# Moving each output store between the two weight loads of a later group in a batched matrix multiplication

**Chip, cores, metric.** One core of one Trainium2 chip. The metric is the device time of one execution in microseconds (us). The kernel before takes 518.66 us (median of six runs, 518.55 to 519.05).

## The reference

```python
x      = randn(8, 16, 256, 512)   # float32
weight = randn(8, 16, 512, 384)   # float32
return np.matmul(x, weight)       # 128 products of 256x512 by 512x384
```

## The kernel before

It works on 32 groups of four products. For each group SP issues two weight loads of 1.57 MB and one x load of 2.10 MB, four groups ahead, and one store of 1.57 MB. (PE also has "weight loads" of its own, called PE loads in the code below: they bring one operand from SBUF into PE.) ACT casts x to bf16, PE transposes it, DVE copies the transposed x out of PSUM and casts the weights, PE multiplies, ACT copies the result out of PSUM.

```python
def load(e, t, U, s):                          # group n
    for d in range(2):                         # two weight loads
        e.wait_ge(w_cast, ...)                 # the slot's weights of group n-2 are cast
        e.dma_start(w_sb[slot][:], ...).then_inc(w_in[slot], 16)
    e.wait_ge(x_cast, ...)                     # x of group n-2 is cast
    e.dma_start(x_sb[s % XS][:], ...).then_inc(x_in[s % XS], 16)

def store(e, t, U, s, pieces=1):
    e.wait_ge(o_copied, ...)                   # the output of group n is copied out
    e.dma_start(out=dram[:, rows], in_=out_sb[s % OS][:, rows]).then_inc(o_out[s % OS], 16)

def on_sync(e):
    for n in range(LAG): load(e, 0, NG, n)     # LAG = 4
    with e.Fori(0, rounds) as t:
        for s in range(U):
            load(e, t, U, LAG + s)             # w, w, x of group n+4
            store(e, t, U, s)                  # store of group n
    ...

def multiply(e, t, U, s):                      # PE, one group
    for q in range(T):                         # 16 transposes, each with its PE load
        e.wait_ge(x_cast, n * T + (q + 1))
        ...
    for q in range(T):                         # 128 multiplications: 32 columns of x,
        for rr in range(2):                    # loaded into PE, by 384 columns of
            for ko in range(KO):               # weights, each with a PE load of its own
                for i in range(G):
                    ins = e.matmul(po[...][mine, rr, :N], x_t[...], w_bf[...][:, ko, :], ...)
```

## Time and profile before

| | before |
|---|---|
| time | 518.66 us |
| span of the profiled execution | 517.2 us |
| busy share: DMA, DVE, PE, ACT | 99.3%, 64%, 59%, 46% |
| moved | 218.1 MB, 429 GB/s in the steady part |

The 16 DMA engines are busy nearly throughout, and no compute engine is. The lines of the profile stand in the prediction. "DMA share" in a row of windows is the mean busy share of the 16 engines, so a single engine working alone shows as 1/16, or 0.06.

### The profile page before, as it was taken

The numbers are of one execution on the slowest core, as the hardware profiler recorded it, in microseconds if no ns is written. First come the engines' busy times: TensorE is split into PE (matmuls) and PEld (weight loads), VectorE is DVE, ScalarE is ACT, GpSimd is POOL, SyncE is SP. The second block draws the span as 40 slices with busy tenths as digits, with TensorE's granted clock in tenths as the row PEclk, the third lists the DMA queues.
The fourth block names the chain that finished last, engine by engine and source line by source line (L and its number), as shares of the span: only waits on it lengthen the run. The fifth ranks groups of instructions, "written<-read, shape, count | busy, mean of one in ns | idle before, by whom it ended". The sixth has DMA issues, their size and how long they took to land.

```text
span 517.2 us, 11523 instructions
## 1 busy us (share of the span) xinstructions
PE 306.6 (59%) x4608; PEld 200.6 (39%) x4608; DVE 332.8 (64%) x384; ACT 236.7 (46%) x264; POOL 0.7 (0%) x6
## 2 busy tenths in 40 slices
PE   0478776556665457645577554776446765467752
PEld 0345444334443334433344332444324443244431
DVE  3698875667556676556675566855658656676550
ACT  0465564443644436435355354454444544544441
POOL 0000000000000000000000000000000000000000
PEclk9998877878777887878777778877788877778777
DMA  8999999999999999999999999999999999999996
GB/s 340 430 423 424 424 432 426 429 428 430 432 427 427 427 428 432 429 427 430 426 431 431 426 429 430 427 432 427 427 429 429 427 433 425 430 428 430 429 428 251
DMA packets 18869, 218.18 MB, mean 422 GB/s; under 512 B 2096, under 2 KB 2096, under 8 KB 2608
## 3 DMA queue, kind: packets, MB, share of 16 engines
q1 hardware_dynamic: 18864, 218.11, 99.3%
q8 instruction: 3, 0.05, 0.0%
q14 instruction: 2, 0.02, 0.0%
HBM read 167.77 MB, written 50.33 MB: 422 GB/s over the span
## 4 chain that ended last, share of the span: by engine, by line
DMA 81%; ACT 10%; PE 4%; issue 3%; ACTq 0%; SPq 0%
DMA x_sb<-in_x_dram 81%; ACT x_bf L132 9%; PE po L180 2%; PE pt L166 1%; ACTq L130 0%; ACT out_sb L194 0%; SPq L111 0%; SPq L103 0%; ACT L132 0%; ACTq L193 0%; SPq L282 0%; SPq L55 0%
## 5 line engine op out<-in xcount | busy, mean ns | idle before, releaser
L147 DVE CAST w_bf<-w_sb 64x1536 bf16<-64x1536 f32 x256 | 244.4, 955 | 47.2 <-DMA w_sb<-in_weight_dram 38.5
L166 PE MATMUL pt<-identity,x_bf 128*128 128x128 f32 x512 | 123.7, 425 | 199.3 <-ACT x_bf L132 199.1
L180 PE MATMUL po<-w_bf,x_t 128*32 128x384 bf16 x4096 | 185.1, 342 | 1.0 <-issue 1.0
L166 PEld LDWEIGHTS pt<-identity,x_bf 128*128 128x128 f32 x512 | 91.8, 216 | 232.1 <-issue 218.3
L194 ACT COPY out_sb<-po 128x768 f32<-128x768 f32 x128 | 102.2, 798 | 147.2 <-PE po L180 147.2
L153 DVE COPY x_t<-pt 128x1024 bf16<-128x1024 bf16 x128 | 88.4, 691 | 122.3 <-PE pt L166 121.8
L132 ACT CAST x_bf<-x_sb 128x1024 bf16<-128x1024 f32 x128 | 124.4, 1042 | 80.9 <-DMA x_sb<-in_x_dram 80.8
L180 PEld LDWEIGHTS po<-w_bf,x_t 128*32 128x32 bf16 x4096 | 108.8, 101 | 73.8 <-issue 14.2
L132 ACT ACT_TABLE_LOAD x8 | 10.3, 1283 | 42.9 <-DMA x_sb<-in_x_dram 42.9
masks.py:199 POOL TENSOR_SCALAR_AFFINE_SELECT identity<-identity 128x128 f32<-128x128 f32 x1 | 0.3, 292 | 0.2 <-POOL identity L200 0.2
L200 POOL MEMSET identity<- 128x128 f32 x1 | 0.2, 204 | 0.5 <-SPq L55 0.5
L271 POOL MEMSET const-bfloat16-1.0<- 128x1 bf16 x1 | 0.1, 101 | 0.0
L271 POOL MEMSET const-uint8-127<- 128x1 uint8 x1 | 0.1, 101 | 0.0
L271 POOL MEMSET const-float32-0.0<- 128x1 f32 x1 | 0.1, 98 | 0.2 <-issue 0.2
L271 POOL MEMSET const-float32-1.0<- 128x1 f32 x1 | 0.1, 98 | 0.0
## 6 DMA issues: line engine op xcount, KB each, us to landing
w_sb<-in_weight_dram SPq DMA_DIRECT2D x64, 1536.0 KB, 27.5
x_sb<-in_x_dram SPq DMA_DIRECT2D x32, 2048.0 KB, 27.5
out_dram<-out_sb SPq DMA_DIRECT2D x31, 1536.0 KB, 30.7
out_dram<-out_sb SPq DMA_DIRECT2D x4, 384.0 KB, 5.9
```

Source lines behind the costliest of these rows:

```text
L132: e.copy(out=x_bf[s % BS][:, rows], in_=x_sb[s % XS][:, rows].rearrange("p r (q s c) -> p r s q c", s=S, c=KO),).then_inc(x_cast, 1)
L147: e.tensor_copy(out=w_bf[(s * G + d * D + a) % WBS][h * HP : (h + 1) * HP], in_=w_sb[slot][a * HP : (a + 1) * HP, h * KO : (h + 1) * KO, : ...
L153: e.tensor_copy(out=x_t[s % TS][:, 2 * q : 2 * q + 2], in_=pt[(s * T + q) % PT][:].bitcast(bf16),).then_inc(t_copied, 1)
L166: ins = e.transpose(pt[(s * T + q) % PT][:, rr, h, :], words[:, 2 * q + rr, h :: KO // 2], identity[:],)
L180: ins = e.matmul(po[(s * T + q) % PO][mine, rr, :N], x_t[s % TS][:, 2 * q + rr, ko // 2, mine, ko % 2], w_bf[(s * G + i) % WBS][:, ko, :], ...
L194: e.copy(out=out_sb[s % OS][:, 2 * q : 2 * q + 2, :], in_=po[(s * T + q) % PO][:, :, :N],).then_inc(o_copied, 1)
L200: e.memset(identity[:], 0.0).then_inc(id_done, 1)
L271: nc = _bacc.Bacc("TRN2", target_bir_lowering=False, num_devices=1)
```

## The change

The intent: a store should stand in the queue with a weight load on either side, and no x load next to it. So the loader is split, and the store goes between the two weight loads of the group issued beside it. For the last groups the old order stays.

```diff
-    def load(e, t, U, s):
+    def load_w(e, t, U, s, d):        # one weight load
+    def load_x(e, t, U, s):           # the x load
 ...
-        rounds = (NG - LAG) // U
+        rounds = (NG - LAG) // U - 1
         with e.Fori(0, rounds) as t:
             for s in range(U):
-                load(e, t, U, LAG + s)
+                load_w(e, t, U, LAG + s, 0)
                 store(e, t, U, s)
+                load_w(e, t, U, LAG + s, 1)
+                load_x(e, t, U, LAG + s)
         for n in range(rounds * U, NG):
+            late = n + LAG >= NG - 1          # then the store comes after the loads, as before
 ...
```

More of the change, by code (lines that the diff above doesn't have):

```diff
@@ L94 @@
     BIAS = 8
-    def load(e, t, U, s):
+    def load_w(e, t, U, s, d):
         n = t * U + s
-        for d in range(G // D):
-            slot = (s * (G // D) + d) % WS
-            if not isinstance(n, int) or n >= 2:
-                e.wait_ge(w_cast, n * (G * S) + ((d + 1) * D * S - 2 * G * S))
-            e.dma_start(
-                w_sb[slot][:],
-                w_rows[bass.ds(n * (G * K) + d * (D * K), D * K)].rearrange(
-                    "(p k) n -> p k n", k=S * KO
-                ),
-            ).then_inc(w_in[slot], 16)
+        slot = (s * (G // D) + d) % WS
+        if not isinstance(n, int) or n >= 2:
+            e.wait_ge(w_cast, n * (G * S) + ((d + 1) * D * S - 2 * G * S))
+        e.dma_start(
+            w_sb[slot][:],
+            w_rows[bass.ds(n * (G * K) + d * (D * K), D * K)].rearrange(
+                "(p k) n -> p k n", k=S * KO
+            ),
+        ).then_inc(w_in[slot], 16)
+    def load_x(e, t, U, s):
+        n = t * U + s
         if not isinstance(n, int) or n >= XS:
@@ L207, in on_sync @@
         for n in range(LAG):
-            load(e, 0, NG, n)
-        rounds = (NG - LAG) // U
+            load_w(e, 0, NG, n, 0)
+            load_w(e, 0, NG, n, 1)
+            load_x(e, 0, NG, n)
+        rounds = (NG - LAG) // U - 1
         with e.Fori(0, rounds) as t:
             for s in range(U):
-                load(e, t, U, LAG + s)
+                load_w(e, t, U, LAG + s, 0)
                 store(e, t, U, s)
+                load_w(e, t, U, LAG + s, 1)
+                load_x(e, t, U, LAG + s)
         for n in range(rounds * U, NG):
+            late = n + LAG >= NG - 1
             if n + LAG < NG:
-                load(e, 0, NG, n + LAG)
-            store(e, 0, NG, n, T if n == NG - 1 else 1)
+                load_w(e, 0, NG, n + LAG, 0)
+                if not late:
+                    store(e, 0, NG, n)
+                load_w(e, 0, NG, n + LAG, 1)
+                load_x(e, 0, NG, n + LAG)
+            if late:
+                store(e, 0, NG, n, T if n == NG - 1 else 1)
         for s in range(OS):
```

## The prediction

> **What bounds the kernel now.** I read the page first: the row of busy times, the two DMA rows of the 40 slices and the table of DMA queues.
>
> ```profile
> span 517.2 us, 11523 instructions
> PE 306.6 (59%) x4608; PEld 200.6 (39%) x4608; DVE 332.8 (64%) x384; ACT 236.7 (46%) x264; POOL 0.7 (0%) x6
> DMA  8999999999999999999999999999999999999996
> GB/s 340 430 423 424 424 432 426 429 428 430 432 427 427 427 428 432 429 427 430 426 431 431 426 429 430 427 432 427 427 429 429 427 433 425 430 428 430 429 428 251
> q1 hardware_dynamic: 18864, 218.11, 99.3%
> ```
>
> No compute engine is busy for more than 64% of the span. The 16 DMA engines are busy for 99.3% of it, and the rate is level from the second slice to the last but one. So the question is not which engine waits, but whether the DMA queue ever runs dry. Next I read the windows (columns: stretch, its length, busy time of PE, PEld, DVE, ACT and POOL, granted clock, DMA share, GB/s), in the steady part and in single microseconds at the end:
>
> ```profile
> 100.00:200.00 100.00, 60.36 (x880) 40.35 (x878) 64.47 (x75) 47.32 (x53) 0.00 (x0) 0.77 1.01 429
> 300.00:400.00 100.00, 57.86 (x884) 37.99 (x872) 66.52 (x77) 46.06 (x52) 0.00 (x0) 0.80 1.01 429
> ...
> 510.00:511.00 1.00, 0.00 (x0) 0.00 (x0) 0.00 (x0) 0.00 (x0) 0.00 (x0) 1.00 1.02 412
> 511.00:512.00 1.00, 0.00 (x0) 0.00 (x0) 0.00 (x0) 0.00 (x0) 0.00 (x0) 0.70 0.67 270
> 512.00:513.00 1.00, 0.00 (x0) 0.00 (x0) 0.00 (x0) 0.00 (x0) 0.00 (x0) 0.50 0.28 111
> 513.00:514.00 1.00, 0.00 (x0) 0.00 (x0) 0.00 (x0) 0.00 (x0) 0.00 (x0) 0.50 0.16 65
> ```
>
> The share is full (1.01) in the steady part and still full in 510 to 511 us. After that it falls off as the engines finish one by one. The landing records say the same: the sixteen parts of the last store arrive over some 4 us, and the slowest of the engines, which is about 2 us behind the first early in the run and over 3 us behind late in it, has work without a gap to the end. The idle of the DMA is thus two scraps: about 2 us before the first packet, and the falling end.
>
> The chain of work that ended last puts 81% on the loads of x. That is time in the queue, not a slow load: the view of the tile x_sb has this line.
>
> ```profile
> DMA to landing us min/median/max: 15.4/27.5/27.8
> ```
>
> An x load of 2.1 MB needs 2.1/0.427 = 4.9 us of the engines and lands 27.5 us after its issue. The other 22.6 us are queue ahead of it, about 9.7 MB, nearly one and a half groups of 6.82 MB (two weight loads of 1.57 MB, x 2.10, store 1.57). So SP issues far ahead of need. Last, SP's own waits in 60 to 460 us and its timeline in one steady group:
>
> ```profile
> SPq L103 <- DVE w_bf L147: 223.7, 50, 6.2
> SPq L111 <- ACT x_bf L132: 107.8, 25, 5.4
> ...
> 237.03 4.26 SPq L103 DMA_DIRECT2D w_sb<-in_weight_dram  x2
> 245.57 0.33 SPq L111 DMA_DIRECT2D x_sb<-in_x_dram  x1
> 246.20 0.36 SPq L122 DMA_DIRECT2D out_dram<-out_sb  x1
> 252.86 0.33 SPq L103 DMA_DIRECT2D w_sb<-in_weight_dram  x1
> ```
>
> SP waits only for free w and x buffers. The store at line 122 is never waited for there: its data has long been made when SP comes to it.
>
> **What the Trainium skill says.** "DMA: Bandwidth & Descriptors", section "Where 436 GB/s comes from", puts the ceiling of a core's 16 engines at 435 GB/s; the steady 429 is 98.6% of that. "HBM Reference", section "Specifications (TRN2)", says that a core streaming alone measures about 425 GB/s, bounded by its DMA engines; the trace agrees with 422 over the span. "DMA: Bandwidth & Descriptors", section "Queues, rings and completion order", says that each engine consumes the descriptors of a queue in ring order. The trace agrees: every x load of the steady part lands within 27.5 to 27.8 us of its issue, as a first-in first-out line would have it. The same page, section "Anatomy of one DMA", says that waits on semaphores are held by the issuing sequencer and not by the DMA engines. So a store moved ahead of a load can hold back that load if its own data is late. That is the one danger of this change, and I work it out below.
>
> **The change, part by part.**
>
> *Removed and added work: none.* The same 64 weight loads, 32 x loads and stores of the same shapes are issued from the same engine, with the same waits on the same values. The bytes stay 218.1 MB. The packet records give 460 ns for a 12 KB packet and 613 ns for one of 16 KB, so 26.7 bytes per ns for both kinds: an engine moves a byte of x as fast as a byte of w or of the output. The order of loads does not alter this price.
>
> *The neighbours of a store.* From the landing records (first engine of each transfer) a weight load costs 3.69 us, an x load 4.88, a store behind x 3.72, and a weight load behind a store 3.59. So the passage from store to load gains 0.1 us, perhaps by overlap. Before, a group is 3.59 + 3.69 + 4.88 + 3.72 = 15.88 us. After, there is still one store in each group, with one passage into it and one out of it: 3.69 + 3.72 + 3.59 + 4.88 = 15.88 us. If going in behind w rather than x is worth the 0.03 us by which that store exceeds a plain 1.57 MB load, 27 moved stores give 27 x 0.03 = 0.8 us. I count half of a possible 0.8 as nothing.
>
> *The store's wait.* In the timeline near the end, the first weight load of group 31 goes out at 460.25 us. The store that would follow it in the new order is of a group whose output copies ended at about 445.0 us (ACT is idle for 3.76 us before its next work at 448.76). So the wait passes with some 15 us to spare, and the second weight load, 4 us later behind its cast, is not held back. Cost: 0.
>
> *Arrival times.* In the line, the store's 3.7 us now lie between the two weight halves and no longer between x and the next weights. So the first half arrives 3.7 us after x, where it came 7.3 us after, and the second at 11.0 us, as now. DVE is free 5.9 us after x has landed (its last x_t copy). It now waits some 1.4 us for the first half; it will then start at once, finish four casts (3.8 us) at 9.7, and wait 1.3 us for the second half. The wait moves; it stays under the 15.9 us period. Weight buffers of the first half come free about 1.5 us sooner. Everything off DMA has slack, so this is worth 0.
>
> *The end.* From group 27 on the store stays behind the loads. Ahead of the last x load lie the same bytes as before, so it should land at 496.6 us again. The x of group 30 lands about 3.7 us later relative to it (one store less in between): 484.3 instead of 480.6. Its copies out then end at about 496.5 instead of 492.8, and DVE's last eight casts at about 498 instead of 496. Both are on time for the transposes of the last group, whose first copy is at 499.0. Even a slip is covered: on the slowest engine the last piece of the last store, issued at 507.7, is reached only at about 515. Cost: 0.
>
> *The sum:* 518.77 - 0 to 0.8 = about 518.6 us. Check from below: 218.1 MB at 429 GB/s is 508.4 us; with about 2 us of start, 5 us of uneven end and closing, and the 1.6 us by which the timed runs exceed the profiled span, that is some 517 to 518.
>
> **The rivals.**
> *The queue was starved and the new order fills it.* Then X waiting for ACT at line 111 (107.8 us of SP's time) would hold back stores that could have filled gaps. For it: stores really do go out 9 us sooner. Against it: share 1.01 in every steady window. At best it takes the scraps, some 2 us: 516.5.
> *A mixture of reads and writes runs better or worse.* Stretches of loads alone ran at 424 (slices 3 and 4), mixed ones at 429. If placing the store among 12 KB packets doubled the gain of 0.1 us per store: 32 x 0.1 = 3 us, 515.6. If it lost it: 522. Against it: the number of passages is the same.
> *The store's wait blocks SP.* If output were late by several microseconds per group, the loads would slip. Against it: 15 us of spare time, and over 20 us of queue that would have to drain first. If the queue did drain for 1 us per group: 546. I give it a hundredth.
> *The uneven end changes.* If the slowest DMA engine gets a smaller or larger lag (now about 4 us): plus or minus 1 us.
>
> **Range and chances.** Runs of the kernel before spread by 0.3 us. The first two rivals and the last allow about a microsecond to either side: 517.7 to 519.5. Faster by 2% would need under 508.4 us, less than the bytes take at the steady rate together with any start and end; slower by 2% needs a drained queue. Hence 0.01, 0.98, 0.01.
>
> **What would show it.** Right: DMA share 99% and 427 to 431 GB/s in the steady windows, x to landing still about 27.5 us, no wait of the store's line in the steady part of SP's waits, stores issued some 9 us sooner, and DVE's weight casts split into four and four with a wait of about 1 us between. Wrong: a slice with DMA share under 0.98 in the middle, an SP wait for ACT's output copies in the loop, or a packet time other than 460 and 613 ns.

## More of the kernel before

The runs were spread over several chips; a run of the kernel before went along on each.

## The result

The changed kernel takes 522.55 us (median of six runs, 522.17 to 523.14), against 518.66 us. The ratio is 1.0074, with a 95% interval of 1.0061 to 1.0087. (A ratio here is the mean time of one kernel's fast runs over that of the other's in the same rounds, so not quite the ratio of the medians.) It is 3.9 us slower. That is within 2%, as forecast, but outside the range of 517.7 to 519.5 us. A change that adds and removes no transfer cost 0.7%.

The page of the changed kernel, the same rows as shown of before:

```profile
span 520.8 us, 11473 instructions
...
DMA  8999999999999999999999999999999999999993
GB/s 335 434 424 424 421 430 428 429 431 432 423 430 429 427 431 432 423 429 432 429 429 428 426 428 429 433 427 428 432 427 426 437 424 425 431 431 430 424 424 144
...
q1 hardware_dynamic: 18864, 218.11, 98.7%
```

The rate is what it was in every slice but the last, which moves 144 GB/s where it moved 251. The windows say the same (stretch, length, busy time of PE, PEld, DVE, ACT and POOL, granted clock, DMA share, GB/s):

```profile
100.00:200.00 100.00, 58.11 (x864) 37.92 (x864) 63.97 (x74) 45.91 (x51) 0.00 (x0) 0.78 1.01 428
300.00:400.00 100.00, 58.67 (x908) 38.80 (x901) 63.92 (x74) 45.92 (x51) 0.00 (x0) 0.80 1.01 429
...
505.00:510.00 5.00, 5.00 (x99) 2.83 (x101) 0.92 (x2) 1.60 (x2) 0.00 (x0) 0.81 0.72 303
...
514.00:515.00 1.00, 0.00 (x0) 0.00 (x0) 0.00 (x0) 0.00 (x0) 0.00 (x0) 0.50 0.24 95
515.00:516.00 1.00, 0.00 (x0) 0.00 (x0) 0.00 (x0) 0.00 (x0) 0.00 (x0) 0.50 0.05 22
516.00:517.00 1.00, 0.00 (x0) 0.00 (x0) 0.00 (x0) 0.00 (x0) 0.00 (x0) 0.50 0.07 28
517.00:518.00 1.00, 0.00 (x0) 0.00 (x0) 0.00 (x0) 0.00 (x0) 0.00 (x0) 0.50 0.06 25
518.00:519.00 1.00, 0.00 (x0) 0.00 (x0) 0.00 (x0) 0.00 (x0) 0.00 (x0) 0.50 0.06 25
```

The steady part looks untouched. The end does not. From 505 us on most engines are already short of work, and for the last four microseconds the share is 0.05 to 0.07: one engine of sixteen is at work and the other fifteen are done. So the lost time is not in the sum of the work but in its spread over the engines. In 505 to 510 us the others run out of stores because the last group starts late. Its x load shows in the chain of waits (start, duration, what), the first line of the kernel before, the second of the changed one:

```profile
468.88 27.67 DMA x_sb<-in_x_dram
```

```profile
475.71 24.48 DMA x_sb<-in_x_dram
```

A load has landed when its slowest engine has delivered. That was at 468.88 + 27.67 = 496.55 us, and is now at 475.71 + 24.48 = 500.19 us, 3.6 us later, with the same bytes ahead of it.

**Which engine, and in which transfers.** The trace keeps the arrival of each of the sixteen parts of a transfer at its semaphore. Subtracting the arrivals of the transfer before, rank by rank, gives what each transfer cost on each engine. For a late store (fastest engine first, slowest last; worked out from the arrival records, us):

```
before,  store of group 25: 3.65 3.64 3.66 3.65 3.66 3.67 3.71 3.67 3.68 3.67 3.67 3.67 3.70 3.70 3.71 3.75
changed, store of group 22: 3.66 3.65 3.64 3.64 3.71 3.71 3.69 3.68 3.68 3.69 3.67 3.67 3.69 3.71 3.71 4.04
```

Fifteen engines take the same time in both. The last takes 3.75 us before and 4.04 us after (one of the larger values; the late stores of the changed kernel lie between 3.81 and 4.04 us). In the loads hardly anything of the kind shows: about 4.9 us for x on every engine. (The weight load behind a store takes the last engine 3.67 to 3.68 us and the middle ones 3.61 to 3.62, alike in both kernels.) The lag of the last engine behind the first was 2.11 us at the first store and 3.48 us at the 28th in the kernel before. In the changed kernel it was 2.74 and 7.30 us. The growth is 1.37 us against 4.56 us, 3.2 us more. With the 0.6 us of different starting lag that is 3.8 us, which accounts for the 3.6 us by which x lands later and by which the two profiled runs differ (522.62 and 518.98 us). (The records don't name the engines. Early in the run another engine is the last, with a constant lag. The one that loses time in stores starts further ahead and overtakes it, at about 230 us in the changed kernel; this is read from the continuity of the ranks. Followed in this way, the losing engine itself is fourth from last at the first store, 0.88 us behind the first engine before and 0.80 us changed, and it loses 2.6 and 6.5 us up to the 28th. So the different starting lag belongs to another engine, and the whole 3.9 us of difference arises in the run.)

**What runs beside those stores.** Compute of a group begins when x has landed on the slowest engine. In the old order that engine's store follows directly behind x. In the new order it follows a weight load later, 3.7 to 7.4 us after the landing. The timelines of one late group, before and changed (start, duration, engine, line, operation, count, idle before; the last line of the kernel before is cut short by the window):

```profile
432.80 3.89 ACT L132 CAST x_bf<-x_sb 128x1024 bf16<-128x1024 f32 x4 [4.31 <-DMA x_sb<-in_x_dram]
433.98 3.96 PE L166 MATMUL pt<-identity,x_bf 128*128 128x128 f32 x16 [6.34 <-ACT x_bf L132]
437.87 2.37 PE L180 MATMUL po<-w_bf,x_t 128*32 128x384 bf16 x32
```

```profile
423.42 3.89 ACT L134 CAST x_bf<-x_sb 128x1024 bf16<-128x1024 f32 x4 [5.34 <-DMA x_sb<-in_x_dram]
424.60 3.96 PE L168 MATMUL pt<-identity,x_bf 128*128 128x128 f32 x16 [7.37 <-ACT x_bf L134]
...
428.48 5.38 PE L182 MATMUL po<-w_bf,x_t 128*32 128x384 bf16 x128
```

Before, the store of the slowest engine lies at about 432.8 to 436.5 us, beside the 16 transposes. Changed, it lies at about 427.0 to 431 us, where PE starts 128 multiplications with as many weight loads within 5.4 us. That gave the first theory: the store of one DMA engine is slowed by compute that runs at the same time. The rival: a store is slow because of what stands beside it in the queue. And the plain control: the new program, not the order.

### The profile page after: what moved, and what is told of

Its sections match the earlier page's. It is cut to its first block, busy times and chain, and to the rows that moved or that the text cites. A ratio compares the mean times of both kernels' runs of the same rounds, so it can differ in the third digit from the quotient of the medians.

```text
span 520.8 us, 11473 instructions
## 1 busy us (share of the span) xinstructions
PE 303.5 (58%) x4608; PEld 200.5 (38%) x4608; DVE 332.6 (64%) x384; ACT 237.0 (45%) x264; POOL 0.7 (0%) x6
## 3 DMA queue, kind: packets, MB, share of 16 engines
q1 hardware_dynamic: 18864, 218.11, 98.7%
## 4 chain that ended last, share of the span: by engine, by line
DMA 81%; ACT 10%; PE 3%; issue 3%; ACTq 0%; SPq 0%
DMA x_sb<-in_x_dram 81%; ACT x_bf L134 10%; PE po L182 2%; PE pt L168 1%; ACTq L132 0%; SPq L113 0%; ACT out_sb L196 0%; SPq L102 0%; ACTq L195 0%; ACT L134 0%; SPq L295 0%; SPq L55 0%
## 5 line engine op out<-in xcount | busy, mean ns | idle before, releaser
L182 PE MATMUL po<-w_bf,x_t 128*32 128x384 bf16 x4096 | 182.3, 339 | 0.0
## 6 DMA issues: line engine op xcount, KB each, us to landing
x_sb<-in_x_dram SPq DMA_DIRECT2D x32, 2048.0 KB, 27.6
```

Of the source, the lines that this page charges most:

```text
L182: ins = e.matmul(po[(s * T + q) % PO][mine, rr, :N], x_t[s % TS][:, 2 * q + rr, ko // 2, mine, ko % 2], w_bf[(s * G + i) % WBS][:, ko, :], ...
```

## The experiments

Thirteen kernels ran. "Share of a store" is the time of a store on the slowest engine, mean over the 18th to the 27th store of a run, worked out as above. In the table, "instructions meanwhile" counts the records of all engines between the start and the end of that share (of PE alone in brackets), from the trace.

In the rows l and a another engine, which loses nothing, is the last one for most of these stores. There the losing engine is followed by its rank instead (fourth from last): stores 4 to 20 of l, 9 to 16 of a.

| kernel | time, us | before on the same chip | share of a store, us | instructions meanwhile |
|---|---|---|---|---|
| l: old order, compute later | 518.76 | 518.50 | 3.71 | 14 (0) |
| before | 518.66 | | 3.75 | 38 (26) |
| a: old order, new program | 518.58 | 518.29 | 3.73 | 29 (16) |
| h: new order, compute later | 520.66 | 518.77 | 3.74 | 38 (29) |
| f: store ahead of x, fewer PE instructions | 520.52 | 518.77 | 3.79 | 32 (22) |
| k: old order, tiny PE instructions added | 522.26 | 518.64 | 3.84 | 74 (62) |
| c: new order, fewer PE instructions | 521.04 | 518.29 | 3.87 | 89 (72) |
| d: new order, less DVE | 522.83 | 518.29 | 3.90 | 129 (114) |
| m: old order, GpSimd counting | 759.86 (see there) | 518.50 | 3.91 | 86 (27) |
| changed | 522.55 | 518.66 | 3.92 | 136 (122) |
| g: store ahead of x, short multiplications | 527.34 | 518.77 | 4.00 | 87 (76) |
| b: store ahead of x | 529.66 | 518.29 | 4.14 | 186 (173) |
| e: store ahead of x, smaller copies | 530.00 | 518.77 | 4.15 | 186 (172) |

### a_oldorder: the new program with the old order

```diff
-                load_w(e, t, U, LAG + s, 0)
-                store(e, t, U, s)
-                load_w(e, t, U, LAG + s, 1)
-                load_x(e, t, U, LAG + s)
+                load_w(e, t, U, LAG + s, 0)
+                load_w(e, t, U, LAG + s, 1)
+                load_x(e, t, U, LAG + s)
+                store(e, t, U, s)
```

> The changed program (its split loader, its loop of six rounds and its longer unrolled end) with the old order of issues: w, w, x, store. What the landing records of the changed kernel show: one of the 16 DMA engines falls behind the others by about 0.25 us with each store (3.9 us for its share of a store, the others 3.65), and ends about 8 us after the first, where before it lost about 0.07 us a store and ended about 4 us after. If the order of the issues does this, this run takes 518.7 us, as before. If it is the new program (code layout, instruction fetches), it takes 522.5 us.

518.58 us, ratio 1.0002 (0.9985 to 1.0019). The program is cleared; the order of the issues is the cause.

### b_before_x: the store between the second weight load and x

```diff
-                store(e, t, U, s)
                 load_w(e, t, U, LAG + s, 1)
+                store(e, t, U, s)
                 load_x(e, t, U, LAG + s)
```

> The store between the second weight load and the x load (w, w, store, x). Theory 1, collision with compute: the straggling engine's share of a store is slow when it runs while PE multiplies and DVE casts, which starts some 4 us after x has landed; here its store runs from 7 to 11 us after x, still beside the casts and multiplications, so 521 to 523 us. Theory 2, neighbours in the queue: the store is slow when neither neighbour is an x load; here one neighbour is, as before, so 518.5 to 519.5 us.

529.66 us, ratio 1.0215 (1.0198 to 1.0232): slower than either theory said. The theory of the neighbours fails as it was stated, since x stands next to the store as it did before (though now behind it; h, k and m settle what stands ahead of it). The direction of the first theory holds, but it was sized too small, because I had taken the loss as the same anywhere beside compute. The share of a store is 4.14 us: here it lies 7.4 to 11 us after x, and PE issues 173 instructions meanwhile, against 122. The lag of the slowest engine reaches 14.9 us at the 28th store, and the other engines sit dry before the last group has even begun. The windows of this run show it:

```profile
505.00:510.00 5.00, 2.75 (x49) 1.68 (x41) 4.22 (x5) 3.80 (x5) 0.00 (x0) 0.89 0.43 182
...
507.00:508.00 1.00, 0.00 (x0) 0.00 (x0) 0.97 (x2) 0.78 (x2) 0.00 (x0) 1.00 0.06 25
```

At 507 us one engine alone is working off its lag, and PE waits for it.

### c_less_pe and d_less_dve: which engine's work collides

```diff
# c_less_pe: one contraction step of four (wrong on purpose)
-                for ko in range(KO):
+                for ko in range(1):
-                            stop=(ko == KO - 1),
+                            stop=True,
# d_less_dve: a quarter of the weight casts, all multiplications (wrong on purpose)
-                        out=w_bf[...][h * HP : (h + 1) * HP],
-                        in_=w_sb[slot][..., h * KO : (h + 1) * KO, :],
+                        out=w_bf[...][h * HP : (h + 1) * HP, 0:1],
+                        in_=w_sb[slot][..., h * KO : h * KO + 1, :],
-                            w_bf[(s * G + i) % WBS][:, ko, :],
+                            w_bf[(s * G + i) % WBS][:, 0, :],
```

> The changed order with a quarter of the multiplications (only the first of four contraction steps; the result is wrong on purpose). DMA still bounds. Theory 1 with PE as the one that collides: the loss per store shrinks and the time falls to 518.5 to 519.5 us. Theory 1 with DVE, and theory 2: unchanged, 522 to 523 us.

> The changed order with a quarter of the weight casts' elements on DVE and all multiplications (each contraction step uses the same columns; the result is wrong on purpose). Theory 1 with DVE as the one that collides: the time falls to 518.5 to 519.5 us. Theory 1 with PE, and theory 2: 522 to 523 us. Weight buffers also come free sooner, which no theory expects to matter.

d: 522.83 us, as without the edit, so the data that DVE's casts move are not it. c: 521.04 us, faster than the changed kernel but not all the way to 519. Less PE work helps; the run missed both of its stated values. Since the copies of ACT moved with the multiplications in c, it could not tell PE from ACT. The next three runs could, and they use the order of b, where the loss is largest.

### e_x_less_copy, f_x_less_pe, g_x_short_pe: ACT's copies, PE's instructions, PE's data

```diff
# e_x_less_copy: 16 of 384 columns (wrong on purpose; the output tiles are zeroed once)
-            out=out_sb[s % OS][:, 2 * q : 2 * q + 2, :],
-            in_=po[(s * T + q) % PO][:, :, :N],
+            out=out_sb[s % OS][:, 2 * q : 2 * q + 2, :16],
+            in_=po[(s * T + q) % PO][:, :, :16],
# f_x_less_pe: the edit of c_less_pe on b_before_x
# g_x_short_pe: as many multiplications, 96 columns each (wrong on purpose)
-                            po[...][mine, rr, :N],
+                            po[...][mine, rr, ko * 96 : ko * 96 + 96],
-                            w_bf[...][:, ko, :],
-                            start=(ko == 0),
-                            stop=(ko == KO - 1),
+                            w_bf[...][:, ko, :96],
+                            start=True,
+                            stop=True,
```

> The order w, w, store, x (529.7 us, the slowest so far), with ACT's copies out of PSUM cut to 16 of 384 columns (wrong on purpose; the output tiles are zeroed once at the start). In that order the straggling engine's share of a store takes 4.05 to 4.2 us and lies 7.4 to 11 us after the landing of x, beside the second half of the multiplications and the last three of ACT's four copies. If ACT's copies are what slows it, the loss of about 0.45 us a store nearly goes: 518.5 to 520.5 us. If PE's multiplications are, or the place in the queue as such: 528 to 530 us.

> The order w, w, store, x with a quarter of the multiplications and of the weight loads of PE (wrong on purpose), all of ACT's copies. If PE is what slows the straggling engine's store: 519 to 522 us, a loss of 0.05 to 0.15 us a store. If ACT's copies are: they now come about 1 us sooner, but still beside the store: 525 to 530 us. If the place in the queue as such: 529 to 530 us.

> The order w, w, store, x with the same number of multiplications and weight loads, each with 96 columns in place of 384 (wrong on purpose). If the number of PE instructions in a time is what slows the store: as slow as with 384 columns or slower, 528 to 532 us. If the columns that PE streams out of SBUF are: 519 to 523 us. If ACT's copies are: 525 to 530 us.

e: 530.00 us, as b, so the data that ACT's copies move have no part in it (there are as many copies as before). f: 520.52 us, 9.1 us faster than b; a quarter of PE's multiplications takes away most of the loss, in the middle of its forecast. g: 527.34 us. With a quarter of the columns streamed but all instructions kept, only 2.3 us of those 9.1 us come back. So it is chiefly the number of PE's instructions, not the data they stream. The time came out just under the forecast for that (it lies in the forecast for ACT's copies too, but e has ruled those out), and some of the instructions now fall outside the store (76 of PE's meanwhile, where b has 173), while the share stays at 4.00 us.

### h_delayed: more work, moved out of the store's way

```diff
         if q == 0:
+            for k in range(3):        # three useless copies on ACT ahead of the casts
+                e.wait_ge(spared, n * 3 + (k + BIAS))
+                e.copy(out=spare[:], in_=x_sb[...]...).then_inc(spared, 1)
```

> The changed order (w, store, w, x), correct, with three useless copies on ACT ahead of the casts of each group: all of the group's work on ACT, PE and DVE after the landing of x starts about 3.3 us later, and the multiplications and copies out then start after the straggling engine's store (3.7 to 7.4 us after x) is over. Collision in time with the multiplications or copies out: the loss of 0.25 us a store falls to 0.05 to 0.1, and the kernel with more work is the faster one, 518.5 to 520 us. The place in the queue, its neighbours or addresses: unchanged, 522 to 523 us.

520.66 us, against 522.55 without the useless work. The store's share falls from 3.92 to 3.74 us, as the theory says, and this is the new order with all of its neighbours and addresses. The lag still grows by 2.6 us up to the 28th store, 0.10 us a store and so at the upper end of the forecast loss, against 1.4 us before and 4.6 us changed. The timeline of this run shows the delay:

```profile
421.80 3.20 ACT L139 COPY spare<-x_sb 128x1024 f32<-128x1024 f32 x3 [1.28 <-DMA x_sb<-in_x_dram]
424.90 3.88 ACT L140 CAST x_bf<-x_sb 128x1024 bf16<-128x1024 f32 x4
...
429.97 6.06 PE L188 MATMUL po<-w_bf,x_t 128*32 128x384 bf16 x128
```

The multiplications begin 8.4 us after x has landed (at 421.60 us), when the slowest engine's store is over. The time missed the forecast by 0.7 us. The last group, too, is made some 3 us later in this kernel. In its last microseconds most DMA engines wait for the final pieces, a cost I had left out.

### k_pe_tiny: adding PE instructions to the kernel before

```diff
+            for _ in range(12):       # ahead of each quarter of the transposes, old order
+                e.matmul(po[0][0:C, 0, 480:484], ..., start=True, stop=True)   # 4 columns
```

> The kernel before (old order), correct, with 12 tiny multiplications on PE (a weight tile of 128x32, 4 columns, into unused columns of PSUM) ahead of each quarter of a group's transposes. They run 1 to 5 us after x has landed, beside the straggling engine's store, 48 multiplications and 48 weight loads a group, and move almost no data. If the number of PE instructions slows that store: its loss grows from 0.06 to about 0.25 us, and the time to 521 to 524 us. If the data that PE streams does: no change, 518.5 to 519.5 us.

522.26 us, ratio 1.0069 (1.0052 to 1.0086), within the forecast. The old order, made slow: 48 tiny multiplications a group, with their weight loads, beside the store. They move almost no data and cost as much as the whole change did. The share of a store rises from 3.75 to 3.84 us. That is a loss of some 0.15 us against the other engines' 3.69, where I had expected 0.25. But here the losing engine is the last one from about the sixth store on (in the changed kernel from the twelfth), and at the 28th it is 7.2 us behind the first engine, as in the changed kernel (7.3).

### i_pool_tiny and m_pool_counts: instructions of another engine

```diff
# i_pool_tiny, on the kernel before
+        with e.Fori(0, 180) as t:
+            e.wait_ge(tinied, t + BIAS)
+            for k in range(64): e.memset(tiny[:, k : k + 1], 0.0)
+            e.drain().then_inc(tinied, 1)
# m_pool_counts, on the kernel before
+        with e.Fori(0, 140) as t:
+            for k in range(64): e.sem_inc(counted[k % 32], 1)
```

> The kernel before (old order), correct, with a stream of some 11,500 tiny GpSimd instructions (each zeroes one column of a spare tile) beside it all through the run. The runs so far: the straggling DMA engine's loss per store follows the number of PE instructions that run beside the store. If it is the number of instructions, whatever the engine, each store now meets some 50 to 100 more and the loss grows from 0.06 to 0.15 to 0.3 us a store: 521 to 526 us. If it is something that only PE does, 518.5 to 519 us.

699.31 us, and no test at all, as its page shows:

```profile
PE 339.8 (49%) x4608; PEld 207.6 (30%) x4608; DVE 616.9 (88%) x384; ACT 235.3 (34%) x264; POOL 411.7 (59%) x11526
```

DVE is busy for 617 us where it was 333 us with the same 384 instructions: the stream of GpSimd writes held up the casts, and DMA no longer bounds. So it was tried again with instructions that touch no memory.

> The kernel before (old order), correct, with a stream of 8,960 semaphore increments on GpSimd, which touch no memory of DVE's. If any engine's instructions slow the straggling engine's store, it meets 50 or more of them in each store: its loss grows from 0.06 to 0.15 to 0.3 us, and the time to 521 to 524 us. If only PE's do: 518.3 to 519 us.

The time of 759.86 us means nothing, since the stream outlasts the kernel; SP's waits say so in one line of 235 us:

```profile
SPq L55 <- POOLq L55: 235.3, 1, 235.3
```

The work of the kernel itself can be read, because DMA bounds it as before (all windows from 100 to 480 us have a share of 1.01 and 429 GB/s). It goes on past 520 us:

```profile
515.00:516.00 1.00, 0.00 (x0) 0.00 (x0) 0.00 (x0) 0.00 (x0) 0.00 (x0) 1.00 0.06 25
...
518.00:519.00 1.00, 0.00 (x0) 0.00 (x0) 0.00 (x0) 0.00 (x0) 0.00 (x0) 0.50 0.06 25
519.00:520.00 1.00, 0.00 (x0) 0.00 (x0) 0.00 (x0) 0.00 (x0) 0.00 (x0) 0.50 0.06 25
```

The signature is that of the changed kernel: one engine alone for five microseconds. Counted from the first arrival of the first load to the last arrival of the last store, this run takes 514.1 us and the kernel before 509.2 us. The increments cost 4.9 us. The share of a store is 3.91 us with 86 instructions meanwhile, only 27 of them PE's. So PE is not special. Semaphore increments on an otherwise idle engine, which read and write no tile, do the same.

### j_first_x_15 and l_old_delayed: two tries at a faster kernel

```diff
# j_first_x_15, on the kernel before: the first x load only
+            e.dma_start(x_sb[0][120:128], rows[120:128]).then_inc(x_part, 16)
+            e.dma_start(x_sb[0][0:120], rows[0:120]).then_inc(x_in[0], 16)
# l_old_delayed, on the kernel before: two useless copies on ACT, as in h_delayed
```

> A try at a faster kernel, correct: the kernel before, but its first x load goes in two pieces, 120 partitions (15 DMA engines, if they are taken from the lowest number up as the other transfers' 16 parts suggest) and 8 partitions (8 engines). One engine of the sixteen then has 4.9 us less to move. If that engine is the straggler, which ends some 4 us after the first and 2 us after most, the time falls by 1.5 to 2.5 us: 516 to 517.2 us. If it is another engine: 518.5 to 519.5 us.

526.30 us. The split load itself is the cost. While it runs, in 13 to 26 us, the rate is about half:

```profile
13.00:26.00 13.00, 0.00 (x0) 0.00 (x0) 3.85 (x5) 0.00 (x0) 0.00 (x0) 1.00 0.99 222
```

One engine gets some 5 us ahead as planned, but another starts 9 us behind that one, some 4 us behind most. Both forecasts are missed, and which engine loses in stores stays unknown. A side result: with that other engine as the slowest, x lands later than the losing engine's store, and no store share above 3.70 us is left on the slowest engine.

> A try at a faster kernel, correct: the kernel before (old order) with two useless copies on ACT ahead of the casts of each group, so that the transposes too start after most of the straggling engine's store (0 to 3.7 us after x). If PE's 32 transposing instructions are what still costs 0.06 us a store there, the loss goes to 0 to 0.03: 27 x 0.05 = 1.3 us gained, and the end, whose multiplications now meet two other stores, costs the same as before or 0.5 us more: 517.3 to 518.3 us against 518.6. If the last store, made 2.2 us later, sets the end: 519 to 520 us.

518.76 us, ratio 1.0005 (0.9991 to 1.0018): no gain, where 0.3 to 1.3 us was forecast. The loop's loss shrinks, but it doesn't go: the losing engine takes 3.71 us a store with 14 instructions meanwhile, and falls behind the first engine by 0.06 us a store, where it was 0.09 us in the kernel before. (The last engine takes 3.70 us a store until the 26th, but it is another one.) In the one trace of each, that other engine was already 2.9 us behind at the first store, where it was 2.1 us in the kernel before, and the stores after the last load, which now meet the last multiplications, lose some 0.9 us as before. Nothing here beats the kernel before.

### What the runs say together

The share of a store on the losing engine rises with the number of instructions that all engines together execute meanwhile: 3.71 us with 14, 3.75 with 38, 3.91 with 86, 3.92 with 136, 4.14 with 186. From end to end that is some 2.5 ns for each. In between the count alone does not set the share: the six runs with 74 to 136 instructions lie at 3.84 to 4.00 us out of order, with g (4.00 us with 87) highest.

The packet records, read after the runs, show the same without the arrivals, and explain g. In 80 to 500 us the kernel before has 2 packets of 12 KB that took over 485 ns, of some 10,200. The changed kernel has 73, and 72 of them lie in the stores of the slowest engine (counted from 0.6 us before each share, since a packet ends about 0.5 us before its arrival is recorded), which make up a quarter of that time; it has no packet of 16 KB over 640 ns, so the loads of x are spared. b has 185, and there the eight packets of the store of group 11 stand out in a row, each beginning where the last ended: 502, 512, 526, 521, 521, 540, 545 and 521 ns in place of 460. These long packets exceed the usual time by 50 ns on average in the changed kernel, with 21 instructions begun during each, by 63 ns with 27 in b, 36 with 12 in m, 67 with 20 in k and 130 with 40 in g. That is 2.4 to 3.4 ns an instruction (c, d and f give 2.2 to 4.5). In g the few packets that still meet PE's instructions meet them more densely.

The orders differ in what they place beside the store: 26, 122 or 173 instructions of PE.

The end of each run shows it once more inside one kernel. In the kernel before, after the last x load, four stores follow each other on the slowest engine. They cost 3.75, 4.04, 4.00 and 3.71 us: the first lies beside the transposes, the next two beside the multiplications, the last after them.

Two things stay open. Why one engine of sixteen, and why only its stores: no run shows what an instruction sends past that engine, be it its fetching or its recording. All these executions were recorded (each lists the core's span and clock), so a run without any recording might behave differently, and I have none.

## Why the prediction was wrong, point by point

- *What bounds the kernel:* right. DMA bounds both kernels, at 429 GB/s.
- *Removed and added work, none:* right as a count, 218.11 MB in 18,864 packets in both.
- *"The order of loads does not alter this price":* this is the step that failed. The price was taken from the usual packet, 460 ns for 12 KB. On one engine the price of a store depends on what is executed meanwhile, and the order decides that. Its share went from 3.75 to 3.92 us on average, and the lag of the last engine grew by 4.56 us over 27 stores and not by 1.37. The prediction took its costs of stores and loads from the first engine of each transfer, where this loss cannot be seen.
- *The neighbours of a store* (0 to 0.8 us gained): no such gain shows. Neighbours are not what slows the store either: with the new neighbours h loses little, and with the old ones k and m lose much.
- *The store's wait, cost 0:* right. SP's waits between 60 and 460 us, and its timeline:

```profile
SPq L102 <- DVE w_bf L149: 224.0, 50, 5.6
SPq L113 <- ACT x_bf L134: 111.3, 24, 5.7
SPq L124 <- ACT out_sb L196: 0.2, 1, 0.2
```

```profile
239.34 0.33 SPq L102 DMA_DIRECT2D w_sb<-in_weight_dram  x1
239.97 0.35 SPq L124 DMA_DIRECT2D out_dram<-out_sb  x1
244.78 0.33 SPq L102 DMA_DIRECT2D w_sb<-in_weight_dram  x1
```

  The store goes out directly behind the first weight load, and waited once, for 0.2 us.
- *Arrival times:* right to about a tenth. The casts split into four and four with a wait of 1.43 us between them, where 1.3 us was worked out:

```profile
429.31 3.92 DVE L149 CAST w_bf<-w_sb 64x1536 bf16<-64x1536 f32 x4
434.66 3.91 DVE L149 CAST w_bf<-w_sb 64x1536 bf16<-64x1536 f32 x4 [1.43 <-DMA w_sb<-in_weight_dram]
```

- *The end, "Cost: 0":* wrong, by the same failed step. The last x was to land at 496.6 us and lands at 500.2.
- *The rivals:* the fourth, a changed lag of the slowest engine, named the right place and was sized at plus or minus 1 us; it measured 3.8 us (8.16 us behind the first engine at the last whole store, against 4.37). The prediction had seen that this engine is 2 us behind early and over 3 us late, and did not ask in which transfers it lost that. The other three did not come about.
- *What would show it:* the marks of being right were found, DMA share, rate, x to landing (27.6 us at the median), no store wait but the one of 0.2 us, casts in halves, and the time was still wrong. Each of them is a mean or a typical value over sixteen engines, and 0.24 us lost in 15.9 us on one engine of sixteen (3.92 us against 3.68) is 0.1% of the whole. But one mark of being wrong was there too, "a packet time other than 460 and 613 ns": the usual packet is unchanged, and the 73 long ones among some 10,100 are the loss itself.
- *Two slips in the working:* not "every" x load of the steady part lands after 27.5 to 27.8 us; every fourth one takes 26.3 to 26.5, since SP issues it later. And 518.77 less 0 to 0.8 us is 518.0 to 518.8, with its middle at 518.4 and not 518.6. Neither changes the verdict.

## What to carry to other kernels

A transfer has landed when its slowest engine has delivered, so in a kernel bound by DMA read the spread of the sixteen arrivals, not only the mean rate; a share of 0.06 at the end is one engine working alone. Where stores can go at more than one place in the queue, try the place where the fewest instructions execute, here directly behind the load that starts the compute. A reordering that moves no byte more can still cost time by what it places side by side, so ask of each moved transfer what will run beside it on its slowest engine. And make sure that it is one engine that you follow: the last arrival can belong to another one, as in l.

## What the Trainium skill lacked or had wrong

- No page says that a DMA engine's stores slow down with the number of instructions executed beside them. On the losing engine a store of 1.57 MB took 3.71 us with 14 instructions meanwhile and 4.14 us with 186, and even semaphore increments on GpSimd counted (3.91 us with 86).
- "DMA: Bandwidth & Descriptors", section "Latency and other measured facts", says that two of the engines are usually slower and, as a best guess, ties this to transfers issued from GpSimd. All loads and stores here were issued from SP, and one engine still fell 4.4 us (before) to 15.7 us (b) behind the first. The records don't name it, so whether it is one of those two is open.
- "Perfetto Trace Analysis", section "Identifying the Most-Contended Engine", tells the reader to judge DMA by its utilization of HBM first, and then to find which DMA resource binds. The first figure is the same 429 GB/s in the steady part of both kernels, 0.7% apart in time; the lag of a single engine, which made the difference, had to be read from the arrivals.
- No page says what splitting a 128-partition load into 120 and 8 partitions costs. Here the rate fell to 222 GB/s while it ran, against 431 GB/s for the whole load in the same stretch.
